# A diffusion-transformer layer in float32: weights split into high and low halves in one step per transfer, up to 1024 columns, with three buffers of 1024

## The chip, the cores and the metric

The kernel runs on one core of a Trainium2 chip. A core has a matrix engine (TensorE, PE in the profile, with its weight loads shown apart as PEld), VectorE (DVE), ScalarE (ACT), GpSimd (POOL), SyncE (SP, which here only issues transfers), and 16 DMA engines. The engines run independent instruction queues, each in order, and wait for each other through semaphores. The metric is the device time of one execution in microseconds, the median of several.

## The reference

One layer with a GLA branch (gated linear attention, forward and backward, 8 heads), a differential-attention branch (8 heads), a gated merge, and a gated MLP with a width-3 convolution. 256 latent and 256 context tokens, model width 2048, MLP width 5632, everything in float32.

```python
h_l = modulate(rms_norm(x, norm1_w), sh1, sc1)          # and h_c from ctx
gq, gk, gv, gr, gaf, gab, dq, dk, dv = split(h @ w_in)
o_lf, _ = gla_scan(aq_l, ak_l, av_l, alf_l, s_cf)       # and backward, after the context's states
o_diff = softmax(q0 k0) v - lam * softmax(q1 k1) v      # keys of context and latent
g_a, g_b = split(sigmoid(h_l @ w_gate + b_gate))
mix = (g_a * (ya @ w_proj_gla) + g_b * (yb @ w_proj_diff)) @ w_out
x_new = x + g1 * mix
h2 = modulate(rms_norm(x_new, norm2_w), sh2, sc2)
out = x_new + g2 * ((silu(conv(h2 @ w_up)[gate]) * conv(...)[val]) @ w_down)
```

The modulation vectors `sh1 ... g2` come from `silu(c) @ w_ada + b_ada`, a matrix of 2048 x 12288.

## The kernel before

Every large product is made from halves. A float32 weight tile is copied by ACT into a reduced format (`whi`, the high half), and DVE, or now and then POOL, subtracts that from the weight to get the rest (`wlo`, the low half). Activations are kept as halves too. A product is then high x high, high x low and low x high, all accumulated in PSUM. Where both halves of the activations stand side by side, the first two are one matmul of 512 columns, and the third is one of 256.

`split` (line 207) does this. Its two tiles come from rings in the pool `stream`: four buffers of 512 columns for `hi`, four for `lo`. The raw weights come by `fetch` (line 230) into a ring of four buffers of 1024 columns, 512 KB each, issued on SP. So one transfer has two splits in most places:

- `col_tile` (line 244) makes one 128-row output tile over 16 k-tiles: two transfers, four splits, each followed by four high and four low matmuls in an order such as h0 l0 h1 l1. Gate, up, mix, the two projections, `gq`, `gr` and `dq` use it.
- `col_tile2` and `gv_chunk`, `dv_chunk` (values, with the weights as the moving operand), the first up tiles (line 1252 on) and `pieces` (line 1374, the down projection) do the same in their own forms.
- the sweep (line 400 on), the first stage, streams 16 k-tiles of input weights, 896 columns each, together with the first modulation matrix: `load_ada` and `load_halves` fetch it in pieces of 512 KB into `SLOTS` = 11 buffers named `ada`. PE multiplies most of it; for three of the k-tiles DVE forms dot products instead (`run_dots`, line 418), with `junk` as a place to throw the products away. All work of this stage keeps program order.

After the sweep a planner orders the work: it places every instruction of each engine by estimated times before the program runs, and blocks marked as high priority are drawn forward. The four GLA head pairs (`gla_pair`, line 791) are such blocks. Each starts with two matmuls `z` for the decays, then has a long chain on ACT, DVE and POOL, and three groups of score matmuls (`sc`, line 873) with the transposes `kT` and the states in between, and at last the outputs `o`. Each score level has a tile `e`, made by four POOL steps (lines 907 to 910), an exponential on ACT (911) and a product on DVE (912). The tiles `e` come from a ring of four. Between these pieces PE works on projections (`gvb`, `dk`, `gk`, `gq`, `gr`, `dvb`), and how much of that stands ahead of each waiting matmul was fixed by the planner.

`ada_next` brings the rest of the modulation matrix as `araw` transfers, one dot product on DVE for each. In the up stage `splits[1] = PSH2` gives every fourth low half to POOL.

```python
hi = st.tile([P, 512], F32R, tag="hi", bufs=4, name="whi")
lo = st.tile([P, 512], F32R, tag="lo", bufs=4, name="wlo")
copied[0] = S.copy(hi[:, :n], raw)
...
e = G if splits[1] and splits[0] % splits[1] == 0 else V
```

Of the kernel before, what the change touches and what calls it, by code (L numbers as in the profile page):

```python
# [18 lines left out]
P = 128  # L19
# [22 lines left out]
CONVS = 7  # L42
SLOTS = 11
DOT_TILES = 7, 11, 15
# [108 lines left out]
def layer_kernel(tc, I, out):  # L153
# [3 lines left out]
    with es:  # L157
# [49 lines left out]
        def split(raw, n, lows=None):  # L207


            hi = st.tile([P, 512], F32R, tag="hi", bufs=4, name="whi")  # L210
            lo = st.tile([P, 512], F32R, tag="lo", bufs=4, name="wlo")
            copied[0] = S.copy(hi[:, :n], raw)  # L212
            if pin[0]:
                tc.keep_in_program_order(copied[0])
            splits[0] += 1
            e = G if splits[1] and splits[0] % splits[1] == 0 else V

            def low():
                i = e.tensor_tensor(lo[:, :n], raw, hi[:, :n].bitcast(F32), op=ALU.subtract)  # L219
                if pin[0]:  # L220
                    tc.keep_in_program_order(i)
                if e is V:
                    copied[1] = i

            if lows is None:
                low()
            else:
                lows.append(low)
            return hi, lo
# [14 lines left out]
        def col_tile(src, acts, b, orders=None, adas=0):  # L244
# [9 lines left out]
            for k0 in range(0, nk, 8):  # L254
# [4 lines left out]
                if k0 and adas:  # L259
                    ada_next(adas)  # L260
                for kk in range(0, kn, 4):
                    whi, wlo = split(raw[:, kk * P:(kk + 4) * P], 4 * P)
                    order = orders[(k0 + kk) // 4]
                    for which in order:
                        j = int(which[1])
                        k = k0 + kk + j
                        sl = slice(j * P, (j + 1) * P)
                        first, last = k == 0 and which == "h0", k >= nk - 4 and which == order[-1]
# [109 lines left out]
        with tc.tile_pool(name="first", bufs=1) as p1:  # L378
# [21 lines left out]
            cbc = p1.tile([P, D], F32, name="cbc")  # L400
            junk = p1.tile([P, 1024], F32, name="junk")
            sums2 = p1.tile([P, len(DOT_TILES), 2, 2, 2], F32, name="sums2")
# [153 lines left out]
            def sweep_splits(k, lows=None):  # L556
                n = 32 + C0
                raw = raws1.pop(k)
                return split(raw[:, :n], n, lows), split(raw[:, n:SWW], SWW - n, lows)

# [167 lines left out]
        with tc.tile_pool(name="gla", bufs=1) as pg:  # L728
# [6 lines left out]
            def gv_chunk(j):  # L735
                banks = [acc_bank("gvb") for _ in range(4)]
                o = C0 + CR * j

                def emptied(t):
                    (V.tensor_copy if t % 2 else S.copy)(gv[:, t, o:o + CR], banks[t][:, :CR])  # L740

                for q in range(8):
                    raw = fetch(I["w_gv"][j, q].rearrange("p a b -> p (a b)"), 2 * CR)
                    ada_next(0.75)
                    ws = [(2 * q + a, lambda a=a: split(raw[:, a * CR:(a + 1) * CR], CR)) for a in range(2)]
                    value_rows(banks, ws, CR, 0, KT - 1, emptied)
# [15 lines left out]
            def col_tile2(src, b, adas=0):  # L762

                for k0 in range(0, KT, 8):
# [3 lines left out]
                    if k0 and adas:  # L768
                        ada_next(adas)
                    for kk in range(8):  # L770
                        if kk % 4 == 0:
                            whi, wlo = split(raw[:, kk * P:(kk + 4) * P], 512)
                        k = k0 + kk
                        both_tile(b, k, whi, wlo, slice(kk % 4 * P, (kk % 4 + 1) * P), k == 0, k == KT - 1)
                        if k0 and kk == 3:
                            flush(latest)
# [13 lines left out]
            def gla_pair(p):  # L790
# [134 lines left out]
                for n, levels in enumerate(RUNS):  # L925
                    group = ([] if n else whole) + [level(li) for li in levels]
                    if n == 1:
                        sb = scored(group[::-1], states)
                        state = pg.tile([P, 2, DV], F32, tag="state", name="state")
                        S.copy(state.rearrange("p a b -> p (a b)"), sb)  # L930
                    else:
                        scored(group[::-1])
# [4 lines left out]
                for j in range(2):  # L937
# [4 lines left out]
                    for c in range(2):  # L942
                        PE.matmul(obs[j][:, :T], gv[:, c, h * DV:(h + 1) * DV], at[:, j, c, :],
                                  start=False, stop=c == 1)
                    places = None
                    if (p, j) == (NPAIR - 1, 1):
# [61 lines left out]
        with tc.tile_pool(name="diff", bufs=1) as pd:  # L1008
# [11 lines left out]
            def dv_chunk(j):  # L1020
# [7 lines left out]
                for q in turn:  # L1028
                    if q in turn[1:3]:
                        flush((later, latest)[turn.index(q) - 1])  # L1030
                    raw = fetch(I["w_dv"][j, q].rearrange("p a b -> p (a b)"), 1024)
                    ws = []
                    for a in range(2):
                        def halves_of(a=a):
                            if j or q > 1:
                                ada_next(0.5 if j else 1)
                            return split(raw[:, a * 512:(a + 1) * 512], 512)
                        ws.append((2 * q + a, halves_of))
# [214 lines left out]
        for k in range(KT):  # L1253
            raw = fetch(I["w_up0"][k], UPS * P)
            for j in range(UPS):
                if j % 3 == 0:
                    whi, wlo = split(raw[:, j * P:(j + 3) * P], 3 * P)
                sl = slice(j % 3 * P, (j % 3 + 1) * P)
                o = banks[j][:, :T + 2]
# [20 lines left out]
        with tc.tile_pool(name="ffn", bufs=1) as pf:  # L1280
# [93 lines left out]
            def pieces(k):  # L1374

                raw = fetch(I["w_down"][h, k], 1024)
                return [split(raw[:, n * 512:(n + 1) * 512], 512) for n in range(2)]

# [53 lines left out]
```

## Time and profile before

| what | value |
|---|---|
| median of three runs | 1678.12 us (1677.63 to 1679.94) |
| the profiled execution | 1679.49 us |
| its span, first to last instruction | 1677.7 us |
| mean granted PE clock | 0.997 |
| bytes read from HBM | 364.73 MB, 219 GB/s over the span |
| ACT high halves (line 212) | 605.9 us busy, 1004 instructions in the group |
| DVE low halves (line 219) | 636.3 us busy, 932 instructions in the group |

How to read the rows of the profile: a group has its line, its engine, the operation, "output<-inputs" by tile names, the shapes, and after the first bar its busy time in us and the mean of one in ns, after the second the idle time of that engine just before it and what ended it. The page's slices give, for 40 equal parts of the span, the busy share in tenths. A row of windows gives the stretch, its length, the busy time (and number of instructions) of PE, PEld, DVE, ACT and POOL, then the granted clock, the DMA share and GB/s. A row of waits gives who waited for whom, the total, the number of times and the longest. PE's matmuls overlap, so their distance from start to start counts and not their length.

### The profile page before, as it was taken

What the parts mean: (1) busy time and instruction counts of PE and PEld (TensorE: products, weight loads), DVE (VectorE), ACT (ScalarE), POOL (GpSimd) and SP (SyncE); (2) the same over time, 40 slices, a digit from 0 to 9 for tenths busy, and PEclk for the clock granted to TensorE, in tenths of its full rate; (3) what the DMA queues carried; (4) which work ended last, traced back from release to release, by engine and by line L of the source; (5) the groups of instructions that cost most, each with busy time, mean ns of one, the idle gap of its engine ahead of it and who ended that gap; (6) DMA issues with size and microseconds to landing.
All of it is one profiled execution on the core that took longest, in us unless ns stands there. A gap on an engine that the chain in (4) does not pass through costs nothing.

```text
span 1677.7 us, 27375 instructions
## 1 busy us (share of the span) xinstructions
PE 1658.6 (99%) x9476; PEld 1412.4 (84%) x9476; DVE 1308.8 (78%) x2479; ACT 977.1 (58%) x1977; POOL 355.9 (21%) x448
## 2 busy tenths in 40 slices
PE   9999999999999999999999999999999999999998
PEld 6679878877888888888888998888888888888887
DVE  5888877887587988788988897888888787755655
ACT  5335465565356777656766686666666666544443
POOL 0011341432010000001223200222222222684000
PEclk9999999999999999999999999999999999999999
DMA  9996644434765556687887666777777676777664
GB/s 384 408 366 210 201 144 141 133 120 132 257 222 180 187 189 189 208 290 272 272 266 248 181 201 212 235 224 239 241 237 235 224 238 214 210 218 210 216 196 142
DMA packets 111979, 372.86 MB, mean 222 GB/s; under 512 B 14560, under 2 KB 19680, under 8 KB 111840
## 3 DMA queue, kind: packets, MB, share of 16 engines
q1 hardware_dynamic: 102112, 362.51, 65.9%
q0 software_dynamic: 5696, 4.24, 0.9%
q10 hardware_dynamic: 4032, 4.37, 0.8%
q8 instruction: 74, 1.21, 0.3%
q14 instruction: 65, 0.53, 0.1%
HBM read 364.73 MB, written 2.10 MB: 219 GB/s over the span
## 4 chain that ended last, share of the span: by engine, by line
PE 91%; DVE 3%; DMA 2%; ACT 2%; POOL 1%; issue 1%; DVEq 0%; SPq 0%; ACTq 0%; POOLq 0%
PE down L1383 14%; PE upg L270 9%; PE upv L270 9%; PE gate L270 7%; PE upv L272 5%; PE upg L272 5%; PE sweep L383 4%; PE gate L272 4%; PE mix L270 4%; PE mix L272 2%; PE pgb L270 2%; PE pga L270 2%; PE dvb L285 2%; PE dvb L286 2%; PE dvb L287 2%; PE dq L270 1%
## 5 line engine op out<-in xcount | busy, mean ns | idle before, releaser
L212 ACT CAST whi<-wraw 128x512 fp32r<-128x512 f32 (+2 forms) x1004 | 605.9, 609 | 389.6 <-DVE wlo L219 112.3
L219 DVE TENSOR_TENSOR wlo<-wraw,whi 128x512 fp32r<-128x512 f32 (+2 forms) x932 | 636.3, 691 | 215.5 <-ACT whi L212 207.0
L270 PE MATMUL upg<-x,whi 128*128 128x512 f32 x656 | 229.0, 391 | 0.0
L270 PE MATMUL upv<-x,whi 128*128 128x512 f32 x656 | 229.0, 391 | 0.0
L1383 PE MATMUL down<-whi,g 128*128 128x512 f32 x704 | 216.9, 389 | 0.0
L272 PE MATMUL upv<-x,wlo 128*128 128x256 f32 x656 | 182.8, 280 | 0.0
L219 POOL TENSOR_TENSOR wlo<-wraw,whi 128x512 fp32r<-128x512 f32 x72 | 100.5, 1396 | 387.8 <-ACT whi L212 375.1
L272 PE MATMUL upg<-x,wlo 128*128 128x256 f32 x656 | 182.6, 280 | 0.0
L270 PE MATMUL gate<-x,whi 128*128 128x512 f32 x512 | 180.1, 397 | 0.0
L371 DVE CUSTOM_DVE_ANT_0 araw<-araw,cb 128x1024 f32<-128x1024 f32 x128 | 161.9, 1267 | 16.4 <-DMA araw<-in_w_ada 16.3
L1383 PEld LDWEIGHTS down<-whi,g 128*128 128x128 f32 x704 | 132.1, 188 | 27.6
L270 PEld LDWEIGHTS upv<-x,whi 128*128 128x128 f32 x656 | 122.4, 187 | 26.6
L270 PEld LDWEIGHTS upg<-x,whi 128*128 128x128 f32 x656 | 122.4, 187 | 26.5
L272 PE MATMUL gate<-x,wlo 128*128 128x256 f32 x512 | 139.9, 284 | 0.0
L1383 PE MATMUL down<-wlo,g 128*128 128x512 f32 x352 | 136.9, 389 | 0.0
L272 PEld LDWEIGHTS upv<-x,wlo 128*128 128x128 f32 x656 | 123.9, 189 | 0.5
L272 PEld LDWEIGHTS upg<-x,wlo 128*128 128x128 f32 x656 | 123.9, 189 | 0.5
L270 PEld LDWEIGHTS gate<-x,whi 128*128 128x128 f32 x512 | 94.4, 188 | 19.7 <-issue 0.7
L272 PEld LDWEIGHTS gate<-x,wlo 128*128 128x128 f32 x512 | 96.4, 188 | 5.7 <-issue 1.8
L270 PE MATMUL mix<-x,whi 128*128 128x512 f32 x256 | 88.8, 396 | 0.0
L1383 PEld LDWEIGHTS down<-wlo,g 128*128 128x128 f32 x352 | 66.1, 188 | 13.6
L1356 POOL DMA_DIRECT2D row<-turned x128 | 69.5, 551 | 27.7 <-PE down L1383 15.6
(327 smaller groups left out, 3236.5 us busy)
## 6 DMA issues: line engine op xcount, KB each, us to landing
wraw<-in_w_up SPq DMA_DIRECT2D x164, 512.0 KB, 4.5
araw<-in_w_ada SPq DMA_DIRECT2D x128, 512.0 KB, 5.1
wraw<-in_w_down SPq DMA_DIRECT2D x88, 512.0 KB, 4.4
wraw<-in_w_gate SPq DMA_DIRECT2D x64, 512.0 KB, 4.4
wraw<-in_w_in SPq DMA_DIRECT2D x58, 512.0 KB, 4.5
ada<-in_w_ad SPq DMA_DIRECT2D x52, 512.0 KB, 10.0
wraw<-in_w_proj SPq DMA_DIRECT2D x32, 512.0 KB, 4.8
wraw<-in_w_out SPq DMA_DIRECT2D x32, 512.0 KB, 4.9
```

The costliest lines, as they stand in the source:

```text
L212: copied[0] = S.copy(hi[:, :n], raw)
L219: i = e.tensor_tensor(lo[:, :n], raw, hi[:, :n].bitcast(F32), op=ALU.subtract)
L270: i = PE.matmul(b.rearrange("p (a b) -> p a b", a=2), whi[:, sl], acts[k], start=first, stop=last)
L272: i = PE.matmul(b[:, T:], wlo[:, sl], acts[k][:, 1, :], start=False, stop=last)
L285: PE.matmul(o, hi[k][:, ts], whi[:, sl], start=first, stop=False)
L286: PE.matmul(o, lo[k][:, ts], whi[:, sl], start=False, stop=False)
L287: return PE.matmul(o, hi[k][:, ts], wlo[:, sl], start=False, stop=last)
L371: i = V.tensor_tensor_reduce(raw, raw, cb[:, q * 1024:(q + 1) * 1024], 1.0, 0.0, op0=ALU.mult, op1=ALU.add, accum_out=ada2[:, j, q:q + 1])
L383: return kept(PE.matmul(*args, **kw))
L1356: nc.gpsimd.dma_start(to[32 * (q % 4):32 * (q % 4 + 1), :, 32 * p:32 * (p + 1)], turned[32 * p:32 * (p + 1), :, 32 * q:32 * (q + 1)])
L1383: i = PE.matmul(banks[h][t][n], g[:, a, ts], w[n][b], start=k == 0 and (a, b) == (1, 0), stop=k == FT - 1 and b == 1)
```

## The change

`split` takes up to 1024 columns and its rings are three buffers of 1024 instead of four of 512: 12 KB per partition for each half instead of 8. Its callers split a whole transfer in one step and cut the result. Counted in the built programs, ACT has 518 copies on that line instead of 1020, 454 of them 1024 columns wide; DVE has 482 subtractions instead of 948, and POOL 36 instead of 72.

Room for that is made in four places: `SLOTS` goes from 11 to 10; `junk` takes the last activation tile's place, which is not in use yet; the GLA state, and the three tiles of the output's norm, live in buffers of the ring `e`, which keeps its four buffers and now gives out ten tiles per pair instead of eight.

```diff
-SLOTS = 11
+SLOTS = 10
...
-            hi = st.tile([P, 512], F32R, tag="hi", bufs=4, name="whi")
-            lo = st.tile([P, 512], F32R, tag="lo", bufs=4, name="wlo")
+            hi = st.tile([P, 1024], F32R, tag="hi", bufs=3, name="whi")
+            lo = st.tile([P, 1024], F32R, tag="lo", bufs=3, name="wlo")
...
+                whi, wlo = split(raw[:, :kn * P], kn * P)
                 for kk in range(0, kn, 4):
-                    whi, wlo = split(raw[:, kk * P:(kk + 4) * P], 4 * P)
                     order = orders[(k0 + kk) // 4]
...
-                        sl = slice(j * P, (j + 1) * P)
+                        sl = slice((kk + j) * P, (kk + j + 1) * P)
...
-            junk = p1.tile([P, 1024], F32, name="junk")
+            junk = hp.tile([P, 1024], F32, tag=f"x{KT - 1}", name="junk")
...
             def sweep_splits(k, lows=None):
                 n = 32 + C0
-                raw = raws1.pop(k)
-                return split(raw[:, :n], n, lows), split(raw[:, n:SWW], SWW - n, lows)
+                whi, wlo = split(raws1.pop(k)[:, :SWW], SWW, lows)
+                return (whi, wlo), (whi[:, n:], wlo[:, n:])
...
-                    ws = [(2 * q + a, lambda a=a: split(raw[:, a * CR:(a + 1) * CR], CR)) for a in range(2)]
+                    both = split(raw[:, :2 * CR], 2 * CR)
+                    ws = [(2 * q + a, lambda a=a: [w[:, a * CR:(a + 1) * CR] for w in both]) for a in range(2)]
...
-                        state = pg.tile([P, 2, DV], F32, tag="state", name="state")
-                        S.copy(state.rearrange("p a b -> p (a b)"), sb)
+                        kept = pg.tile([P, 2, T], F32, tag="e", bufs=4, name="e")
+                        state = kept[:, 0, :].rearrange("p (a b) -> p a b", a=2)
+                        S.copy(kept[:, 0, :], sb)
...
-                    places = None
+                    if not j:
+                        e = pg.tile([P, 2, T], F32, tag="e", bufs=4, name="e")
+                    places = e[:, 0, :], e[:, 1, :], kept[:, 1, :]
...
-                raw = fetch(I["w_down"][h, k], 1024)
-                return [split(raw[:, n * 512:(n + 1) * 512], 512) for n in range(2)]
+                both = split(fetch(I["w_down"][h, k], 1024), 1024)
+                return [[w[:, n * 512:(n + 1) * 512] for w in both] for n in range(2)]
```

The other edits (`col_tile2`, `dv_chunk`, the first up tiles) are of the same kind.

Since the planner orders the work, the instructions move as well. On ACT, in the fourth pair (pair 3), from the second `z` (its first readers are `m` and `l`) to the exponential `rc` that the scores wait for, there stood before:

```order
L807 ACTIVATE m<-z,nba 128x512
L808 ACTIVATE l<-z,vec 128x512
L212 CAST whi<-wraw 128x512
L809 ACTIVATE l<-l 128x512
L810 ACTIVATE l<-l 128x512
L834 ACTIVATE qe<-bfb,bl 128x128
L896 ACTIVATE e<-bfb,bl 128x128
L971 COPY dk_1358<-nraw 128x256
L895 ACTIVATE e<-bfb 128x128
L836 ACTIVATE qe<-bfb 128x128
L827 ACTIVATE rc<-rc 128x512
```

and now, from the third of these steps on:

```order
L212 CAST whi<-wraw 128x1024
L809 ACTIVATE l<-l 128x512
L834 ACTIVATE qe<-bfb,bl 128x128
L896 ACTIVATE e<-bfb,bl 128x128
L212 CAST whi<-wraw 128x1024
L974 COPY dk_1295<-nraw 128x256
L810 ACTIVATE l<-l 128x512
L281 COPY gr_1287<-gr 128x256
L212 CAST whi<-wraw 128x1024
L895 ACTIVATE e<-bfb 128x128
L836 ACTIVATE qe<-bfb 128x128
L212 CAST whi<-wraw 128x1024
```

with `rc` next. Four copies of 1024 columns stand among these steps where one of 512 stood.

On PE, further on in the same pair, around the transposes `kT` and the second group of scores, before:

```order
L270 MATMUL gr<-x_1279,whi 128x512
L270 MATMUL gr<-x_280,whi 128x512
L848 MATMUL kT<-ident,rc 128x128 x4
L873 MATMUL sc<-e 128x128 x8
L272 MATMUL gr<-x_280,wlo 128x256
```

and now:

```order
L287 MATMUL dvb<-wlo,x_559 128x512
L848 MATMUL kT<-ident,rc 128x128 x4
L285 MATMUL dvb<-whi,x_559 128x512
L286 MATMUL dvb<-whi,x_559 128x512
L287 MATMUL dvb<-wlo,x_559 128x512
L285 MATMUL dvb<-whi,x_559 128x512
L286 MATMUL dvb<-whi,x_559 128x512
L873 MATMUL sc<-e 128x128 x8
L287 MATMUL dvb<-wlo,x_559 128x512
L873 MATMUL sc<-e 128x128 x4
```

Five matmuls have come between the transposes and the scores, and the work around them is `dvb`, a stage that used to begin after this pair. The numbers of other matmuls that stand between a pair's marks, counted from the two programs ("pairs" are a high matmul of 512 columns and a low one of 256, "long" ones have 512 columns, `gvb` ones 272):

| from, to | pair 0 | pair 1 | pair 2 | pair 3 |
|---|---|---|---|---|
| last `z` to first `sc`, before | 114 gvb, 16 pairs | 46 long, 16 pairs | 50 long, 20 pairs | 48 long, 12 pairs |
| now | 120 gvb, 16 pairs | 70 long, 16 pairs | 50 long, 16 pairs | 35 long, 56 pairs |
| first `sc` to `kT`, before | 24 gvb | 21 long | 6 long, 8 pairs | 2 long, 8 pairs |
| now | 24 gvb | 21 long | 5 long, 8 pairs | 21 long |
| second `sc` to last `sc`, before | 34 gvb | 26 long | 25 long | 13 pairs |
| now | 83 gvb | 34 long, 10 pairs | 32 long, 7 pairs | 57 long |
| last `sc` to `o<-at`, before | 16 gvb | 16 long | 7 long, 4 pairs | 8 pairs |
| now | 20 long | 14 long, 1 pair | 2 long, 7 pairs | 16 long |

On DVE, in the up stage, from one low half past the product on `araw` and the gate `g` to the next, before:

```order
L219 TENSOR_TENSOR wlo<-wraw,whi 128x512
L371 ISA araw,ada_77<-araw,cb 128x1024
L371 ISA ada_77 128x1
L238 TENSOR_TENSOR g_13940<-C,g_13940 128x256
L282 TENSOR_TENSOR C<-upg,C 128x256
L219 TENSOR_TENSOR wlo<-wraw,whi 128x512
```

and now:

```order
L371 ISA araw,ada_77<-araw,cb 128x1024
L371 ISA ada_77 128x1
L1297 SCALAR_TENSOR_TENSOR C<-C,vec 128x255
L219 TENSOR_TENSOR wlo<-wraw,whi 128x1024
L1299 SCALAR_TENSOR_TENSOR C<-C,vec 128x255
L282 TENSOR_TENSOR C<-upg,C 128x256
L1307 TENSOR_TENSOR C<-C 128x256
L1297 SCALAR_TENSOR_TENSOR C<-C,vec 128x255
L238 TENSOR_TENSOR g_12539<-C,g_12539 128x256
L1299 SCALAR_TENSOR_TENSOR C<-C,vec 128x255
L219 TENSOR_TENSOR wlo<-wraw,whi 128x1024
```

The convolution's steps stand between two subtractions of 1024 columns, and the product on `araw` stands ahead of the first of them.

More of the change, by code (lines that the diff above doesn't have):

```diff
@@ L769, in col_tile2 @@
                         ada_next(adas)
+                    whi, wlo = split(raw, 1024)
                     for kk in range(8):
-                        if kk % 4 == 0:
-                            whi, wlo = split(raw[:, kk * P:(kk + 4) * P], 512)
                         k = k0 + kk
-                        both_tile(b, k, whi, wlo, slice(kk % 4 * P, (kk % 4 + 1) * P), k == 0, k == KT - 1)
+                        both_tile(b, k, whi, wlo, slice(kk * P, (kk + 1) * P), k == 0, k == KT - 1)
                         if k0 and kk == 3:
@@ L1031, in dv_chunk @@
                     raw = fetch(I["w_dv"][j, q].rearrange("p a b -> p (a b)"), 1024)
+                    both = split(raw, 1024)
                     ws = []
@@ L1036, in halves_of @@
                                 ada_next(0.5 if j else 1)
-                            return split(raw[:, a * 512:(a + 1) * 512], 512)
+                            return [w[:, a * 512:(a + 1) * 512] for w in both]
                         ws.append((2 * q + a, halves_of))
@@ L1254, in layer_kernel @@
             raw = fetch(I["w_up0"][k], UPS * P)
+            whi, wlo = split(raw[:, :UPS * P], UPS * P)
             for j in range(UPS):
-                if j % 3 == 0:
-                    whi, wlo = split(raw[:, j * P:(j + 3) * P], 3 * P)
-                sl = slice(j % 3 * P, (j % 3 + 1) * P)
+                sl = slice(j * P, (j + 1) * P)
                 o = banks[j][:, :T + 2]
```

## The prediction

> **What bounds the kernel now.** I read the page first, then the granted clock, then what TensorE (PE) waited for, and only then the stages.
>
> ```profile
> span 1677.7 us, 27375 instructions
> ...
> PE 1658.6 (99%) x9476; PEld 1412.4 (84%) x9476; DVE 1308.8 (78%) x2479; ACT 977.1 (58%) x1977; POOL 355.9 (21%) x448
> ...
> PEclk9999999999999999999999999999999999999999
> DMA  9996644434765556687887666777777676777664
> ...
> L219 POOL TENSOR_TENSOR wlo<-wraw,whi 128x512 fp32r<-128x512 f32 x72 | 100.5, 1396 | 387.8 <-ACT whi L212 375.1
> ```
>
> PE is busy 99% of the span and holds its clock; VectorE (DVE) is at 78%, ScalarE (ACT) at 58%. The change touches no matmul that counts: the same products run, in pieces of the same size. So cheaper splits are worth nothing by themselves; only PE's pauses can change. All of them that exceed a short latency are in one view, what PE waited for:
>
> ```profile
> PE sc L873 <- DVE e L912: 4.3, 3, 3.1
> PE dk L349 <- DVE wlo L219: 1.7, 1, 1.7
> PE sc L873 <- DVE at L920: 1.5, 2, 0.9
> PE sweep L383 <- ACT x L547: 1.2, 3, 0.5
> PE kT L848 <- ACT at L924: 1.1, 1, 1.1
> PE o L943 <- DVE at L920: 1.1, 1, 1.1
> PE sweep L383 <- DVE ones L176: 1.1, 1, 1.1
> PE sc L873 <- ACT kn L849: 1.0, 2, 0.9
> PE dq L272 <- DVE wlo L219: 0.6, 2, 0.4
> PE ab L529 <- ACT row L520: 0.5, 1, 0.5
> PE ab L383 <- DMA ada<-in_w_ad: 0.2, 1, 0.2
> ```
>
> (Columns: total us, times, longest.) Without the four sweep rows (`sweep`, `ab`) 11.3 us are left, all in the gated-linear-attention (GLA) part and shortly after it. From the first up-projection to the end nothing waits. Only two rows, 1.7 + 0.6 us, wait for a split; the rest waits for GLA's own chain on DVE, ACT and POOL. The longest pause also costs clock:
>
> ```profile
> 372.00:375.50 3.50, 2.96 (x28) 2.96 (x30) 3.50 (x5) 1.69 (x4) 1.65 (x2) 0.51 0.09 16
> 380.00:385.00 5.00, 3.31 (x22) 2.88 (x23) 4.71 (x9) 4.83 (x13) 2.70 (x5) 0.73 0.07 11
> ```
>
> The first number after the five engines is the granted clock: 0.51 behind the 3.1 us pause, 0.73 behind the next two. PE's 2.96 us at half clock would have been about 1.5 us, so that pause cost some 4.6 us. The second stretch loses about 0.27 x 3.31 = 0.9 us. The ceiling for any gain is then 11.3 + 1.5 + 0.9 = 13.7 us.
>
> The Trainium skill, page "TensorE: Matmul & The Clock Gate", section "Part 1: The HAM clock gate (the "warmup" mystery)", says that the clock drops to half after about one idle window of 3.4 us. By that rule a 1 us pause alone would cost no clock, and the 0.9 us would vanish with its neighbours; the trace shows a drop behind pauses of about 1.1 and 0.9 us close together, so I keep the 0.9 us.
>
> **The steady stages: up, down, gate, mix.** Pitches first.
>
> ```profile
> 1200.43 0.39 PE L270 MATMUL upg<-x,whi 128*128 128x512 f32 x1
> 1200.66 0.28 PE L272 MATMUL upg<-x,wlo 128*128 128x256 f32 x1
> 1200.78 0.39 PE L270 MATMUL upg<-x,whi 128*128 128x512 f32 x1
> ...
> 1205.97 0.39 PE L270 MATMUL upv<-x,whi 128*128 128x512 f32 x1
> ```
>
> ```profile
> 1433.55 235.34 PE down L1383 x1038
> ```
>
> A high and a low matmul take 0.35 us together, a tile of 16 such pairs 5.54 us, a 512-column matmul alone 235.34 / 1038 = 0.227 us.
>
> ```profile
> L212 ACT CAST whi<-wraw 128x512 fp32r<-128x512 f32 x924 | 569.7, 620 | 367.9 <-DVE wlo L219 111.3 <-PE upg L270 76.4 <-PE dvb L286 33.6
> L212 ACT CAST whi<-wraw 128x272 fp32r<-128x272 f32 x32 | 12.7, 417 | 9.3 <-PE gvb L286 6.5 <-PE gq L270 1.0 <-DVE wlo L219 1.0
> ```
>
> ```profile
> L219 DVE TENSOR_TENSOR wlo<-wraw,whi 128x512 fp32r<-128x512 f32 x852 | 595.5, 706 | 209.7 <-ACT whi L212 202.4 <-PE dvb L286 2.1 <-PE down L1383 0.7
> L219 DVE TENSOR_TENSOR wlo<-wraw,whi 128x384 fp32r<-128x384 f32 x48 | 26.8, 564 | 4.4 <-ACT whi L212 3.1 <-PE mix L272 0.9
> ```
>
> No 1024-column split is in the trace. The copy's slope is (620 - 417) / 240 = 0.85 ns a column, so 1024 take 620 + 512 x 0.85 = 1.05 us. The subtraction's slope is 142 / 128 = 1.1 ns, so 1.27 us. Bounds: no less than one old piece (0.62, 0.71), no more than two (1.24, 1.41). A split goes from 1.33 to 2.32 us latency. The cover is what PE still has in the other buffers when one comes free: three of 1.39 us before, 4.2 us; two of 2.77 us after, 5.5 us. Spare time goes from 2.8 to 3.2 us, and nothing waited with 2.8. In `down` a split lasts 12 x 0.227 = 2.7 us, the same answer. POOL's split, 36 of 1024 instead of 72 of 512, is sized by POOL's rows:
>
> ```profile
> L908 POOL TENSOR_TENSOR e<-bfb 128x128 f32<-128x128 f32 x28 | 22.9, 818 | 17.4 <-DVE bfb L822 17.4
> L910 POOL TENSOR_TENSOR e<-bfb 128x128 f32<-128x128 f32 x28 | 20.0, 716 | 0.0
> L909 POOL TENSOR_TENSOR e<-bfb 128x128 f32<-128x128 f32 x28 | 19.7, 705 | 0.0
> L907 POOL TENSOR_TENSOR e<-bfb 128x128 f32<-128x128 f32 x28 | 19.6, 701 | 92.9 <-DVE bfb L815 80.5 <-PE sc L873 6.6 <-DVE wlo L219 3.0
> ```
>
> Their mean is 0.735 us at 128 columns; with 1.396 at 512 the slope is 1.72 ns, so 1024 take 2.3 us (between 1.4 and 2.8). 1.05 + 2.3 = 3.4 us under a cover of 5.5. These stages cost **0**, with the slow rival below as the other end.
>
> **GLA, where the sum is made.** The new instruction order puts other amounts of matmul work in front of each waiting matmul; counts are from the built order, durations from the pitches.
>
> ```profile
> 353.90 0.39 PE L803 MATMUL z<-gaT,wa 96*128 96x512 f32 x1
> ...
> 372.54 2.93 PE L873 MATMUL sc<-e 64*128 64x128 f32 x24 [3.12 <-DVE e L912]
> ```
>
> 1. *First scores of pair 3.* Between its second `z` and its first `sc` stood 12 high/low pairs and 48 matmuls of 512: 15.1 us for a chain that took 18.2 (354.3 to 372.5). Now 56 pairs and 33 matmuls stand there, 27 us. The chain grows too: four 1024-column copies now stand before `rc` on ACT where one of 512 stood, 4 x 1.05 - 0.62 = 3.6 us, so 22 us. What those copies wait for is PE's own progress, which needs no cover. Pause gone: -3.1, and -1.5 of clock.
> 2. *First scores of the others.* Pairs 0 and 1 get more in front (120 instead of 114 `gvb`; 70 instead of 46 long matmuls), so their 1.2 us go. Pair 2 loses 1.4 us in front (16 pairs instead of 20) and had nothing to spare: +1.0, between 0 and 1.4.
> 3. *`o<-at`*: 16 short matmuls before, 20 of 512 after (4.5 us): -1.1. *`kT` of pair 3*: 8 pairs and 2 of 512 before (3.3 us), 21 of 512 after (4.8 us): -1.1.
> 4. *`sc` behind `at` and `kn`* (2.5 us): pair 0 has 14 `gvb` in front instead of 19; nothing gained, +0.6.
> 5. *Splits late for `dk` and `dq`* (2.3 us): in `dk` 512 columns feed PE 2.7 us, so the cover rises from 8.2 to 10.9 us while the split's latency rises by 1.0. Spare time +1.7, as much as the long one waited: -1.7, between 0 and -2.3.
> 6. *A new wait.* With two more tiles in the ring of four `e` buffers, the last two levels' factors wait for the second group of scores; before, one of them did. Per pair that is another 4 POOL steps, 2.9 us, then ACT and DVE as below.
>
> ```profile
> L911 ACT ACTIVATE e<-e 128x512 f32<-128x512 f32 x28 | 17.6, 630 | 29.7 <-POOL e L910 29.7
> L912 DVE TENSOR_TENSOR e<-e,qk 128x512 f32<-128x512 f32 x32 | 26.7, 840 | 6.8 <-ACT e L911 6.4
> ```
>
> Two levels are 5.9 + 0.63 + 0.84 = 7.4 us. Behind the waiting POOL step only the same pair's levels are queued. The order now has, in pair 2 (the least), 32 matmuls of 512 and 7 pairs before the last scores, 9.7 us. It hides. With one long split ahead on ACT and one on DVE, 2.3 us, it just fits: 0, at most +1 per pair if the cover is gone.
>
> 7. *The first sweep step*: one 896-column subtraction stands before the low halves of `x` instead of one of 512: +0.4, once. The dot products' scratch moves into the last `x` tile, which DVE first writes a step after its last dot: 0.
> 8. *New misfits.* The order is planned ahead of the chip; four pairs each had a pause of 0.4 to 1 us in it, and a new order will make some of its own: I take +2 (0 to 6).
>
> **Fewer slots.** Ten modulation buffers instead of eleven, in the stage where the DMA engines are full (9996 on the page).
>
> ```profile
> SPq L355 <- DMA ada<-in_w_ad: 41.9, 47, 1.0
> SPq L355 <- PE ab L383: 4.5, 7, 1.9
> ```
>
> SP's queue waits 47 times for an earlier landing and 7 times for PE to free a buffer. As the landings are the limit, a slot less takes nothing: 0, and at most another 4.5 us if each such wait came twice.
>
> **The sum.** -3.1 - 1.5 - 1.2 + 1.0 - 1.1 - 1.1 + 0.6 - 1.7 + 0.4 + 2 = -5.7 us. The profiled execution took 1679.5 us (span 1677.7), 1.4 above the median of 1678.1, so it gives 1673.8 on its own time and **1672.4** against the median.
>
> **Rivals.**
> - *The pauses only move.* GLA's chain is as long as before and every new order has misfits; items 1 to 5 are given back: 1678 +- 3. For it: two old pauses (3.1 and 1.7) came from queues that the planner had misjudged. Against: cover grows in most places.
> - *POOL blocks DVE in the up stage (slower).* One POOL split in four, now 2.3 us at a stretch.
>
> ```profile
> L238 DVE TENSOR_TENSOR g<-C,g 128x256 fp32r<-128x256 f32 x44 | 51.1, 1162 | 0.0
> L238 DVE TENSOR_TENSOR x<-C,x 128x256 fp32r<-128x256 f32 x16 | 6.6, 413 | 0.0
> ```
>
> The same subtraction takes 1162 ns where POOL splits and 413 where it does not. If a block of 2.3 us and the 1.27 us product on `araw` both fall ahead of one DVE split, 3.6 us stand against 3.2 spare: 0.4 us in each of 36 tiles, 14 us, 1692 (at 0.8 us, 1707). It decides from 3.2 us of delay on. Against: the next DVE split's high half comes 2.8 us after POOL's, when the block is over.
>
> The Trainium skill, page "SBUF — State Buffer", section "SBUF: two separate sides", gives the rule: VectorE with two SBUF inputs and GpSimd lock a shared port pair for a whole instruction, and the loser fully blocks. By that rule the block doubles with the piece; the 1162 against 413 ns agree that there is one.
> - *The slots starve the sweep*: +4.5, 1682 where nothing else gains.
> - *The change does not do what it says*, in that the gain is not in the splits at all: that is my forecast, and a trace with the old pauses and some 500 fewer split copies would be the first rival.
>
> **How the numbers follow.** Forecast 0.58, pauses only move 0.27, POOL 0.07, slots or the new `e` wait 0.08. The forecast's own range is 1667 to 1677: item 8 from 0 to 6, items 2 and 5 at their ends. Downward the ceiling of 13.7 us is 1664, which needs every pause gone; I stop at 1666. Upward the range takes in the moving pauses up to 1681; the rest is left out. A measurement of this kernel tells 0.2%, 3.4 us, from no change. Faster than 1674.8: 0.50 of the forecast and 0.08 of the moving pauses, 0.58. Within: 0.29. Slower than 1681.5: 0.13.
>
> **What would show it.** Step 1: no `sc` wait over 1 us near pair 3, and no half clock but at the ends. Step 5: no PE row waiting for `wlo`. Steady stages: still no PE wait, tiles of 5.54 us, ACT copies near 1.05 and DVE 1.27 us, POOL near 2.3. Wrong if `upg` or `upv` wait for `wlo` from POOL or DVE, if the last scores wait for `e` from POOL, or if `ab` waits for its DMA by more than 1 us.

## The result, and the profile after

The changed kernel takes 1675.76 us (1674.64 to 1676.76, 20 runs) against 1678.30 (1676.88 to 1679.94, 20 runs): ratio 0.9985, 95% interval 0.9978 to 0.9992. That is 2.5 us faster where 5.7 were forecast; the direction was right, and 1675.8 lies in the range. The experiments show that this small gain is the rest of two larger effects of opposite sign, which do not simply add, and the prediction had neither at its size.

The page of the changed kernel, the rows that answer to those of before:

```profile
span 1673.9 us, 25645 instructions
...
PE 1657.2 (99%) x9476; PEld 1409.6 (84%) x9476; DVE 1279.7 (76%) x2013; ACT 898.4 (54%) x1475; POOL 338.7 (20%) x412
...
L212 ACT CAST whi<-wraw 128x1024 fp32r<-128x1024 f32 (+3 forms) x502 | 514.5, 1028 | 420.6 <-PE down L1386 138.9
L219 DVE TENSOR_TENSOR wlo<-wraw,whi 128x1024 fp32r<-128x1024 f32 (+3 forms) x466 | 562.9, 1209 | 205.7 <-ACT whi L212 200.5
...
L219 POOL TENSOR_TENSOR wlo<-wraw,whi 128x1024 fp32r<-128x1024 f32 x36 | 86.8, 2411 | 396.3 <-ACT whi L212 396.3
...
L1297 DVE SCALAR_TENSOR_TENSOR C<-C,vec 128x255 f32<-128x255 f32 x88 | 105.5, 1201 | 36.8 <-ACT C L1296 36.8
```

ACT has 79 us less to do and DVE 29, and PE is at 99% as before: none of that work was on the path. The sizes are as estimated: alone, the 1024-column copies take 1.05 us and the subtractions 1.24 (the two rows above mix four widths), and 2.41 on POOL. What PE waits for now, in the same view as before (total us, times, longest):

```profile
PE sc L873 <- DVE e L912: 2.1, 3, 1.6
PE gr L270 <- ACT whi L212: 1.3, 1, 1.3
...
PE dq L270 <- ACT whi L212: 1.0, 2, 0.6
PE kT L848 <- ACT at L924: 1.0, 1, 1.0
PE dvb L285 <- ACT whi L212: 0.8, 1, 0.8
PE sc L873 <- ACT kn L849: 0.7, 1, 0.7
PE gr L272 <- DVE wlo L219: 0.5, 1, 0.5
...
PE sweep L383 <- DVE wlo L219: 0.3, 1, 0.3
```

Outside the sweep it is 8.1 us instead of 11.3 (with three rows of 0.2 and 0.3 us that are not shown). The long pauses of pair 3 are gone, and the clock is full there:

```profile
397.53 1.61 PE L873 MATMUL sc<-e 64*128 64x128 f32 x24
398.97 0.61 PE L873 MATMUL sc<-qk 64*128 64x128 f32 x8
404.42 0.60 PE L848 MATMUL kT<-ident,rc 128*128 128x128 f32 x4
```

```profile
380.00:390.00 10.00, 10.00 (x59) 8.69 (x58) 10.00 (x18) 7.73 (x14) 8.05 (x9) 1.00 0.61 188
390.00:400.00 10.00, 10.00 (x68) 8.27 (x67) 9.31 (x13) 3.70 (x7) 5.47 (x8) 1.00 0.54 161
400.00:410.00 10.00, 10.00 (x74) 7.90 (x73) 8.23 (x14) 4.72 (x9) 5.79 (x10) 1.00 0.63 197
```

The timeline's rows carry no bracket, so nothing was waited for; in the windows the number behind the five engines is the clock. New are waits for **high** halves (`gr`, `dq`, `dvb`: 3.1 us), which the kernel before did not have.

From the first `pga` matmul (758.3 us here, 762.1 before) to the first `down` matmul (1429.6 and 1433.4) pass 671.3 us in both kernels, and 244.3 us from there to the end. The whole difference arises before.

### The profile page after: what moved, and what is told of

It is laid out like the page before. It is cut to its first block, busy times and chain, and to the rows that moved or that the text cites. A ratio compares the mean times of both kernels' runs of the same rounds, so it can differ in the third digit from the quotient of the medians.

```text
span 1673.9 us, 25645 instructions
## 1 busy us (share of the span) xinstructions
PE 1657.2 (99%) x9476; PEld 1409.6 (84%) x9476; DVE 1279.7 (76%) x2013; ACT 898.4 (54%) x1475; POOL 338.7 (20%) x412
## 4 chain that ended last, share of the span: by engine, by line
PE 90%; DVE 4%; DMA 3%; ACT 1%; POOL 1%; issue 1%; DVEq 0%; SPq 0%; ACTq 0%
PE down L1386 14%; PE upg L270 9%; PE upv L270 9%; PE gate L270 7%; PE upv L272 5%; PE upg L272 5%; PE sweep L383 4%; PE gate L272 4%; PE mix L270 4%; PE mix L272 2%; PE pga L270 2%; PE pgb L270 2%; PE dvb L285 1%; PE dvb L287 1%; PE dvb L286 1%; PE dq L270 1%
## 5 line engine op out<-in xcount | busy, mean ns | idle before, releaser
L212 ACT CAST whi<-wraw 128x1024 fp32r<-128x1024 f32 (+3 forms) x502 | 514.5, 1028 | 420.6 <-PE down L1386 138.9
L219 DVE TENSOR_TENSOR wlo<-wraw,whi 128x1024 fp32r<-128x1024 f32 (+3 forms) x466 | 562.9, 1209 | 205.7 <-ACT whi L212 200.5
L219 POOL TENSOR_TENSOR wlo<-wraw,whi 128x1024 fp32r<-128x1024 f32 x36 | 86.8, 2411 | 396.3 <-ACT whi L212 396.3
L1297 DVE SCALAR_TENSOR_TENSOR C<-C,vec 128x255 f32<-128x255 f32 x88 | 105.5, 1201 | 36.8 <-ACT C L1296 36.8
```

What stands on the lines that cost most here:

```text
L1297: V.scalar_tensor_tensor(u[:, 1:], b[:, :T - 1], vcol("conv_w", ct), u[:, 1:], op0=ALU.mult, op1=ALU.add)
```

## The experiments

Twelve kernels ran, each timed in turn with the kernel before on one chip (three jobs, in which the kernel before took 1678.5 to 1678.8 us). "Waits" is the sum of PE's waits outside the sweep in its profile; "pga" the start of the first `pga` matmul; ratios are to before, with 95% intervals.

| | kernel | us | ratio | waits | pga |
|---|---|---|---|---|---|
| | before | 1678.3 | | 11.3 | 762.1 |
| | the change | 1675.76 | 0.9985 [0.9978, 0.9992] | 8.1 | 758.3 |
| 1 | change, norm halves in tiles of their own | 1675.27 | 0.9978 [0.9969, 0.9987] | 8.4 | 756.7 |
| 2 | change, steps of at most 512 columns | 1672.97 | 0.9963 [0.9950, 0.9975] | 6.6 | 756.6 |
| 3 | before, e ring shared | 1670.01 | 0.9947 [0.9934, 0.9959] | 3.3 | 752.5 |
| 4 | before, 10 slots, `junk` moved | 1679.38 | 1.0001 [0.9992, 1.0010] | 11.7 | 762.7 |
| 5 | before, pair 3 later | 1671.45 | 0.9951 [0.9938, 0.9963] | 5.8 | 753.9 |
| 6 | change, e ring not shared | 1680.09 | 1.0008 [0.9999, 1.0017] | 10.0 | 763.8 |
| 7 | 3 and 4 with six buffers of 512 | 1676.08 | 0.9981 [0.9972, 0.9990] | 7.2 | 757.5 |
| 8 | before, two buffers of 1024 | 1771.18 | 1.0546 [1.0531, 1.0560] | 63 | 799.8 |
| 9 | 6 with pair 3 later | 1678.73 | 0.9999 [0.9990, 1.0008] | 9.3 | 762.2 |
| 10 | 3 and 4 | 1669.43 | 0.9947 [0.9934, 0.9961] | 2.3 | 750.9 |
| 11 | change, no subtraction on POOL | 1676.26 | 0.9986 [0.9977, 0.9995] | 7.8 | 758.1 |
| 12 | before, e ring of three | 1672.49 | 0.9963 [0.9951, 0.9976] | 5.8 | 754.4 |

The times follow the waits in the main; runs 6 and 9 are some 2 to 3 us longer than their waits would have it by the other runs, and that time was not located. In each kernel but number 8, 670 to 672 us pass from the first `pga` to the first `down`.

**1 and 2: the late high halves.** In the changed kernel a short split, of the norm's squares `nsq`, takes one of three wide buffers, and long copies queue behind it on ACT:

```profile
451.67 0.41 ACT L212 CAST whi<-nsq 128x256 fp32r<-128x256 f32 x1
451.99 2.12 ACT L212 CAST whi<-wraw 128x1024 fp32r<-128x1024 f32 x2
```

Run 1 gives the norm's halves places of their own (two `dk` tiles not yet in use, and the place of the later tile `osqs`); run 2 keeps the wide buffers and cuts the instructions:

```diff
-            copied[0] = S.copy(hi[:, :n], raw)
+            cuts = [(0, n)] if n <= 512 or pin[0] else [(0, n // 2), (n // 2, n)]
+            for c0, c1 in cuts:
+                copied[0] = S.copy(hi[:, c0:c1], raw[:, c0:c1])
```

(the subtraction in the same way).

> The changed kernel, with the halves of the q/k norms' squares (8 splits of 512 columns, 8 of 256) in tiles of their own instead of in the ring of three buffers of 1024. Theory A (a small split occupies a whole one of three buffers, so less weight is split ahead, and PE waits for the next high half): the new waits of the changed kernel for whi (gr 1.3, dq 1.0, dvb 0.8 us) and the wlo wait of gr (0.5) go, 2 to 4 us off the changed kernel, some 1672.5 us. Theory B (the new waits come from the longer copy itself, 1.03 instead of 0.62 us): they stay, within 1 us of the changed kernel, 1675 to 1677.

> The changed kernel, but outside the sweep each half is again made by two instructions of up to 512 columns, into the same three buffers of 1024. Theory A (the gain is in the order of the work and the pauses of the gated-linear-attention part, none in the number of split instructions): 1674 to 1677, as the changed kernel, unless the planner's order differs much. Theory B (fewer, longer instructions are what pays): back to some 1678.3.

In run 1 the wait of `gr` fell from 1.3 to 0.2 us and those of `dq` and `dvb` to nothing, but the norm's own tiles were waited for in turn, and the time hardly moved (1675.27). The waits went as theory A had it, and the time stayed as theory B had it:

```profile
PE hss L647 <- DVE nhl L238: 4.6, 2, 2.9
PE hss L647 <- DVE wlo L219: 1.3, 1, 1.3
```

Run 2 gained 2.8 us on the change, with waits of 6.6, which is more than either theory had. Its order differs too, so how much of that is the length of a step is not shown; it is not where the large terms are.

**3 and 4: the room made for the buffers, alone.**

```diff
-                        state = pg.tile([P, 2, DV], F32, tag="state", name="state")
+                        kept = pg.tile([P, 2, T], F32, tag="e", bufs=4, name="e")
...
-                    places = None
+                    if not j:
+                        e = pg.tile([P, 2, T], F32, tag="e", bufs=4, name="e")
+                    places = e[:, 0, :], e[:, 1, :], kept[:, 1, :]
```

```diff
-SLOTS = 11
+SLOTS = 10
...
-            junk = p1.tile([P, 1024], F32, name="junk")
+            junk = hp.tile([P, 1024], F32, tag=f"x{KT - 1}", name="junk")
```

> The kernel before, with the state and the output norm's tiles moved into the ring of e tiles as in the change, and nothing else of it. Theory A: more work stands ahead of the last scores, the pauses elsewhere stay as they were, the o wait of 1.1 us may go: 1676.5 to 1679. Theory B (the ring is what moved the pairs and took the pauses away): the whole gain, some 1675.8, with pair 3's pause of 3.1 us gone.

> The kernel before with ten modulation buffers and the dot products' scratch in the last x tile, nothing else of the change. Theory A (landings are the limit, not buffers): 1678.3 within 1 us, ab waits for its DMA by 0.2 us as before. Theory B (the sweep starves): up to 4.5 us more, 1682.8, with ab waiting for DMA.

The sharing of the ring, which the prediction counted as one more wait, takes 8.8 us off the time of before in that job (1678.77), more than three times what the whole change gains, and more than theory B had. The splits there are the old ones. The slots take nothing (theory A), though `ab` waits 0.6 us for its DMA instead of 0.2.

**5: is it the order?** Pair 3 is written later in the program and held back on PE; the ring is as before:

```diff
-            with tc.high_priority(500):
-                gla_pair(3)
...
                 gr_tile(h)
+                if h == 5:
+                    held.append(last_mm[0])
+                    with tc.high_priority(500):
+                        gla_pair(3)
```

and the first score matmul of pair 3 has an order-only edge from `held`.

> The kernel before with one thing changed: the first score products of pair 3 are put behind the last matmul of the sixth gr tile in TensorE's order; splits, halves' buffers and the e ring are as before. Theory A (the ring of e tiles works through TensorE's order: pair 3's first products come later, so their operands are ready, and its two score halves stand closer to what follows): the wait of sc at pair 3 (3.1 us) and the two windows at half clock go, the waits outside the sweep fall from 11.3 us to 5 to 7, time 1672 to 1674, ratio 0.996 to 0.9975. Theory B (the sharing of the ring takes pauses away by something other than order, as by the freed private tiles): order alone brings under 2 us, ratio 0.999 to 1.000. Theory C (the pauses only move): the wait of sc comes back at another row with the same total, 1678.

Theory A held, and its gain was somewhat larger than expected: 7.0 us, with no change to any buffer. Between pair 3's last `z` and its first score stand 58 pairs and 26 long matmuls (counted as in the table of the change), where there stood 12 and 48.

**6, 9 and 8: the wide halves alone.** Run 6 is the change with the state and the output's norm in places of their own (those of `gr3` and `dk7`, not yet in use). Run 9 adds to it the move of run 5, with pair 3's tiles in the ring. Run 8 is the kernel before with the wide steps, two buffers for each half and no other edit.

> The changed kernel (halves of up to 1024 columns in 3 buffers, 10 slots) with the state tiles and the output norm's tiles of the gated attention in places of their own, out of the e ring. The run with the ring's sharing alone gave 1670.0, 8.8 us less than before; the change has both and gave 1675.8. Theory A (the ring's sharing brings the gain and the wide halves cost about 5 us): without the sharing the wide halves stand alone, 1681 to 1685, ratio 1.001 to 1.004. Theory B (both bring a gain, and they overlap): at or below before, 1674 to 1678, ratio 0.997 to 1.000.

> The run with wide halves and private state tiles (1680.1), with pair 3 alone moved: its program place, its first score products' place behind the sixth gr tile on TensorE, and its state tiles in the e ring; pairs 0 to 2 keep their places. On the kernel with narrow halves the same move brought 7.0 us (1678.5 to 1671.5). Theory A (the gain is pair 3's place in TensorE's order, whatever the halves' width): 7 us again, 1672 to 1674, ratio 0.996 to 0.9975; the 2.6 us wait of gr and the sc waits at 390 us go. Theory B (wide halves make new waits where pair 3 now stands, as gr, dq, dvb for their copies): half of the gain or less, 1676 to 1679, ratio 0.9985 to 1.0005.

> The kernel before with halves of up to 1024 columns in two buffers instead of three (as many bytes as before), the rest of its memory as before. My theory (the steady stages cost nothing because two halves of 1024 ahead, 5.5 us, cover a split of 1.03 + 1.21 us, or 1.03 + 2.41 with the subtraction on GpSimd): with one ahead the cover is 2.8 us, less than 3.4 us, so that each of the 36 subtractions on GpSimd makes TensorE wait 0.6 to 2 us in the stage of up products, 20 to 70 us in all, and splits on VectorE behind other work add to it: 1700 to 1760, ratio 1.013 to 1.05. Rival (the splits' engines have time to spare and the planner starts them early enough): within 5 us of the change with its ring taken out, 1678 to 1685.

Wide halves without the ring (run 6) fall between the two theories: no gain, and +1.6 us, with an interval that just reaches no change. The move of pair 3 brought 1.4 us here and not 7 (theory B of run 9): its long wait goes, and 9.3 us of small ones stay. With two buffers (run 8) the cover is gone. The row that was empty in the change is now the largest:

```profile
PE upg L272 <- POOL wlo L219: 17.1, 36, 0.5
PE dvb L285 <- ACT whi L212: 5.1, 3, 3.8
PE dq L272 <- DVE wlo L219: 4.9, 5, 1.5
```

All 36 POOL subtractions are waited for, 0.5 us each; 1.05 + 2.4 us against 2.8 us of cover gives 0.65. It is 93 us slower in all, more than expected and more than the 63 us of waits.

**7 and 10: width or room?** Run 10 is runs 3 and 4 together. Run 7 differs from it in the buffers of the halves alone:

```diff
-            hi = st.tile([P, 512], F32R, tag="hi", bufs=4, name="whi")
-            lo = st.tile([P, 512], F32R, tag="lo", bufs=4, name="wlo")
+            hi = st.tile([P, 512], F32R, tag="hi", bufs=6, name="whi")
+            lo = st.tile([P, 512], F32R, tag="lo", bufs=6, name="wlo")
```

> The kernel before with the e ring shared, 10 slots and the square sums' output in a slot, as in the change, and the halves in steps of 512 columns in 6 buffers of 512: the change's bytes of halves, not its width. Theory A (the price of the change's splits is the width: a first product waits for 1024 columns instead of 512, and a short split takes a whole buffer): no price is left, time as with the ring's sharing alone, 1669 to 1671, ratio 0.994 to 0.9955, waits outside the sweep 3 to 4 us. Theory B (the price comes from splits that run further ahead, as more room lets them, and stand in front of the attention's copies on ScalarE and VectorE): part of it stays, 1672 to 1675, ratio 0.996 to 0.998.

> The ring's sharing (1670.0 alone) together with the 10 slots and the square sums' output in a slot; halves in four buffers of 512 as before. It differs from the run with six buffers of 512 (1676.1) by the two further buffers alone. Theory A (the two further buffers let the splits run ahead and stand in front of the attention's products on VectorE): 1669 to 1671.5, ratio 0.994 to 0.996. Theory B (the slots cost once the ring is shared): 1674 to 1677, ratio 0.997 to 0.9985.

Two more buffers of 512 cost 6.6 us (1669.43 to 1676.08, intervals well apart), and with them the narrow kernel is as slow as the change, which has the same bytes in wide pieces (1676.08 and 1675.76). That is theory B of run 7, a little above its range, and theory A of run 10: a price of this size comes with the **room** alone. That the width has none is not shown by it, since run 2, with the change's buffers and steps of 512 columns, is 2.8 us faster than the change. PE's waits in run 10:

```profile
PE sc L873 <- DVE e L912: 0.6, 2, 0.4
PE dq L272 <- DVE wlo L219: 0.6, 2, 0.4
...
PE gr L272 <- DVE wlo L219: 0.6, 2, 0.3
PE gr L270 <- ACT whi L212: 0.5, 1, 0.5
```

and in run 7:

```profile
PE sc L873 <- DVE e L912: 3.2, 3, 1.4
PE sc L873 <- ACT kn L849: 1.5, 1, 1.5
...
PE o L944 <- DVE at L920: 0.8, 1, 0.8
PE dk L349 <- DVE bl L830: 0.7, 1, 0.7
```

How more room makes one of these scores late is to be seen on ACT in pair 2, from the second `z` to its first reader `m`. Run 10, where that `z` starts at 298.9 us:

```profile
299.98 0.61 ACT L212 CAST whi<-nsq 128x512 fp32r<-128x512 f32 x1
300.49 0.69 ACT L807 ACTIVATE m<-z,nba 128x512 f32<-128x512 f32 x1
301.07 0.69 ACT L808 ACTIVATE l<-z,vec 128x512 f32<-128x512 f32 x1
301.64 0.40 ACT L798 CAST wa<-wr 96x256 fp32r<-96x256 f32 x1
301.93 1.67 ACT L212 CAST whi<-wraw 128x512 fp32r<-128x512 f32 x3
```

Run 7, where it starts at 300.9:

```profile
300.52 0.64 ACT L212 CAST whi<-nsq 128x512 fp32r<-128x512 f32 x1
301.04 2.73 ACT L212 CAST whi<-wraw 128x512 fp32r<-128x512 f32 x5
303.64 0.42 ACT L798 CAST wa<-wr 96x256 fp32r<-96x256 f32 x1
303.94 0.70 ACT L309 ACTIVATE hny<-hss,epsb 128x512 f32<-128x512 f32 x1
304.52 0.63 ACT L212 CAST whi<-wraw 128x512 fp32r<-128x512 f32 x1
305.03 0.33 ACT L833 ACTIVATE qe<-bfb 128x128 f32<-128x128 f32 x1
305.25 0.32 ACT L894 ACTIVATE e<-bfb 128x128 f32<-128x128 f32 x1
305.44 0.70 ACT L807 ACTIVATE m<-z,nba 128x512 f32<-128x512 f32 x1
```

With more buffers the planner puts five copies in a row ahead of the chain; `m` starts 4.5 us after its `z` instead of 1.6, and DVE's last factors `e`, which the scores read, end 21.0 us after the `z` instead of 18.6. PE then stands 0.7 us before pair 2's first scores and not at all in run 10. The other new waits of run 7 (1.5 us for `kn` in pair 2, 1.4 before the last scores of pair 3, 0.7 more in pair 0, 0.8 of `o<-at`, 0.7 of `dk`) come with the same two buffers, but how was not followed. In the changed kernel `m` starts at 311.1 us, 9.4 after its `z`; there it waits for DVE, which between 303.4 and 309.2 us has three subtractions of 1024 columns ahead of the scans that `m` needs.

**12: any wait in the ring?** One number, `bufs=4` to `bufs=3` for the tiles `e` of the kernel before.

> The kernel before with the ring of e tiles cut from four buffers to three; state and output norm keep tiles of their own. In TensorE's order pair 1's products move and pair 3's stay where they were (12 row pairs and 48 long products ahead of its first score products). Theory A (what counts is pair 3's place, and with it the 3.1 us wait and the clock after it): those stay, 1676 to 1680, ratio 0.999 to 1.001. Theory B (any further wait in the ring spreads the products and takes pauses away): a gain of over 3 us, ratio under 0.998.

Theory A fell. Pair 3's wait did stay, shorter, and the clock dropped behind it:

```profile
367.71 2.93 PE L873 MATMUL sc<-e 64*128 64x128 f32 x24 [2.38 <-DVE e L912]
```

```profile
365.00:367.70 2.70, 0.33 (x2) 0.01 (x1) 2.70 (x5) 2.70 (x7) 0.90 (x2) 0.93 0.00 0
367.70:371.20 3.50, 3.49 (x33) 3.37 (x33) 3.50 (x6) 1.06 (x3) 2.17 (x3) 0.56 0.15 50
```

Yet 6.2 us went: the waits of `dk` (1.7), `o<-at` (1.1) and of `sc` behind `at` and `kn` (2.5) are gone, and a new one of `gr` (1.9) has come. Some 3.5 us of waits went from pairs 0 to 2. Pair 3 lost 2.8: its first pause is 0.7 us shorter, and those at its `kT` (1.1) and its second scores (0.9) are gone, and with them the second stretch at half clock. Ten pairs stand between that `kT` and those scores in run 12, where none stood before. So the place of pair 3's first scores is not all that counts, but how the pairs, and the parts within them, are spread among the projections. In the built orders, 46 long matmuls stand between pair 1's last `z` and its first scores before, 81 in run 3 and 83 in run 12; in pair 3 it is 48 long and 12 pairs before and in run 12, 27 and 52 in run 3. Run 5 moves pair 3 alone, run 12 the others and pair 3's second scores, run 3 both, and they gain 7.0, 6.2 and 8.8 us. That a wait in the ring makes the planner put more work in front is read from these orders and wasn't tried apart from them.

**11: POOL's block.**

> The changed kernel with GpSimd's 36 subtractions of the second part of the up products given to VectorE. Theory A (they block VectorE's operations beside them, 1.2 us instead of 0.5 for the gated product, but only in time that VectorE has to spare): that operation falls to about 0.5 us, VectorE's busy time there rises by 36 x 1.2 = 43 us less 36 x 0.7, and the time stays, 1674.5 to 1677, ratio 0.998 to 0.999. Theory B (they hold TensorE up unseen): faster by over 1 us, under 1674. Theory C (VectorE has no such room left without them): waits for low halves appear among the up products, over 1678.

Theory A held: without POOL the product on line 1297 takes 480 ns again, and the time is that of the change.

```profile
L1297 DVE SCALAR_TENSOR_TENSOR C<-C,vec 128x255 f32<-128x255 f32 x88 | 42.1, 480 | 0.0
```

## Why the prediction was right in direction and too large

- *The bound* held. PE is at 99% in both kernels, no time came from 108 us less busy time on ACT and DVE, and only PE's pauses moved.
- *The steady stages at 0* were right, as 671.3 us twice shows; only `gate` has a wait for a half, of 0.2 us. Run 8 shows that the cover is what hides the splits: with two buffers POOL is waited for 36 times.
- *Item 1* (first scores of pair 3, with the clock) was right: no wait at 397.5 us, clock 1.00. That the pause cost clock at all is in part chance: run 4 has the same pause of 3.1 us at full clock (last section). The second stretch at half clock went too, which the sum had not claimed. It lasts from 382.3 to 385.7 us, past the end of the prediction's window at 385.0, and by the same working it cost some 1.7 us, not 0.9.
- *Item 2* read two waits wrongly. It had 1.2 us in the first scores of pairs 0 and 1; in the trace of before, both stand in pair 0 (0.5 us at its first scores, at 175.0 us, and 0.6 at its second, at 183.9), and pair 1's first scores wait for nothing. They fell to 0.3. Pair 2's new wait was put at 1.0 (0 to 1.4); it is 1.6. *Item 3*: both named waits went, but a `kT` wait of 1.0 us came in pair 0. *Item 4* had the wrong sign: 2.5 us fell to 0.7, where 0.6 more had been expected.
- *Item 5* failed. It sized the cover of a split in `dk` and concluded that splits would be late less often: -1.7. The one wait of `dk` went, but all waits for halves outside the sweep rose from 2.3 to 4.0 us, most of it in `gr`, `dq` and `dvb`. What was missed is the queue: the cover counts only if ACT takes the copy up when the buffer comes free, and the norm's short splits take a wide buffer and stand in front (run 1). Its sign, no row of PE that waits for `wlo`, did not come: there are three, 0.9 us in all.
- *Item 6* is the step that failed most. It counted the shared ring as one more wait, priced at nothing as it hides, and looked no further. Alone it is worth -8.8 us (run 3), by the order that it makes the planner choose; order alone, with the ring as it was, brings 7.0 (run 5). In the prediction that gain stood in items 1 to 4 as the new order's, without asking which of the edits made that order.
- *Item 8* was under-sized. It took +2 us for new misfits. The extra room costs 6.6 us where the ring is shared and the steps are of 512 columns (run 10 to 7); that it costs as much in the change is inferred. The two terms do not add: the ring alone -8.8, the wide halves alone +1.6 (run 6), both -2.5 and not -7.2. That the time still came out in the range is luck in part: the gain of the ring and the cost of the room were both put too low, and the errors made up for each other.
- *Item 7* was right: +0.3 for the low half in the sweep. *Fewer slots at 0* was right (run 4), and run 10 keeps run 3's time.
- *POOL as a rival*: the block is there (1201 ns where the same product took 480), but it does not reach PE, and run 11 gains nothing without it. The Trainium skill, page "SBUF — State Buffer", section "SBUF: two separate sides", has it that the loser of the shared port waits for the whole instruction; the trace agrees: of the 88 products on line 1297, 53 take 0.48 us and 35 take 2.2 to 2.6, beside pieces of 2.41 us, and in run 11 all take 0.48.
- *The pauses only move* was half of what happened: 11.3 us fell to 8.1, and 4.3 of those are in rows that were not there before. It goes for the split's part and not for the ring's.

What stays open: the waits fell by 3.2 us and the lost clock, by the working above, by as much again, the medians by 2.5 and the two profiled spans by 3.8; the rest does not stand in the view of waits and was not located. And why run 2 beats run 7, with the same bytes and the same width of step, was not followed up; both orders are the planner's.

Runs 3 and 10 are the best kernels of the study, 1670.0 and 1669.4 us: the change's memory edits without its splits.

## What to carry over

Where one engine is busy all the time and the order is planned ahead, a change of buffers is first a change of order: test its parts one by one, since here the part meant to make room brought 8.8 us and the room itself cost most of that. More buffers are no gain by themselves, because a planner can fill them with work that is not urgent, in front of a chain that is, as in pair 2 of run 7. Price a wait that is added by what it pushes back, not only by whether it hides.

## What the runs showed of the hardware

A pause of 2.4 us was enough to drop the granted clock to a mean of 0.56 over 3.5 us (run 12, above), and one of 2.4 us in run 6 dropped it to 0.54 over 3.0 us. In run 1 a stretch with a wait of 2.9 us left it at 1.00:

```profile
556.00:559.40 3.40, 0.50 (x5) 0.15 (x2) 3.20 (x7) 3.37 (x8) 0.00 (x0) 1.00 0.25 48
559.40:562.00 2.60, 2.60 (x16) 2.28 (x17) 2.60 (x9) 2.42 (x8) 0.00 (x0) 1.00 0.46 178
```

In run 4 the 3.1 us pause of the kernel before, at the same scores, left it at 1.00 too:

```profile
372.27 1.61 PE L873 MATMUL sc<-e 64*128 64x128 f32 x24 [3.13 <-DVE e L912]
```

```profile
367.30:370.70 3.40, 1.84 (x11) 1.33 (x9) 3.18 (x7) 3.13 (x8) 3.40 (x5) 1.00 0.00 0
370.70:374.10 3.40, 1.83 (x32) 1.83 (x32) 3.40 (x5) 2.73 (x6) 1.99 (x4) 1.00 0.00 0
```

So the length of a pause alone does not decide it at this size. What the traces show in its place is a grid: in the records of the granted clock, every stretch at half clock behind a pause lasts 3.41 us (once, in run 4, 6.83), and the changes in one trace lie whole multiples of 3.41 us apart. Run 4's pause falls into two steps of that grid, as the windows show, and PE is busy for 1.8 us of each. In the kernel before, the same pause falls for the most part into one step, 368.6 to 372.0 us, with PE busy for 0.8 us, and the half clock begins at 372.0. The grid lies otherwise in each trace (in run 4 it lies 1.3 us earlier than in the kernel before), so which short pause costs clock is chance here. Cut on that grid, from 10 us on, all traces but that of run 8 agree: PE is busy for at most 1.47 us of each step ahead of a drop from full clock, and for at least 1.57 us of every other step (that one is in run 1, whose pause of 2.9 us also falls into two steps). In run 8 two of the five drops come behind 1.9 and 2.2 us, so the busy time in a step is not the whole rule. The Trainium skill, page "TensorE: Matmul & The Clock Gate", section "Part 1: The HAM clock gate (the "warmup" mystery)", has the clock fall after about one idle window of 3.4 us; the drops behind 2.4 us are earlier than that, and the measurement decides.

In run 8 the up products were slower as well, 397 ns for each high matmul of `upg` instead of 392 in the change, at a granted clock of 1.00; from its start to that of the next matmul it is 236 ns instead of 230 (medians). It is a small part of the 30 us that the waits don't hold; neither its cause nor the rest was looked for.

```profile
L270 PE MATMUL upg<-x,whi 128*128 128x512 f32 x656 | 234.0, 397 | 0.0
```
